# One gelu function at the gMLP projections' eviction, and v's chain ahead of u's half, in a hybrid encoder layer

## The chip, the cores and the metric

The kernel runs on one core of a Trainium2 chip. The metric is the device time of one execution in microseconds (us), the median of three runs. The engines of the core are called as in the profile: PE multiplies matrices (PEld loads its stationary operand), DVE does elementwise work with two operands and reductions, ACT applies functions elementwise with a scale, POOL does small powers here, and SP's queue (SPq) issues nearly all DMAs. Each engine and each queue takes its instructions in the order in which they stand in the program.

## The reference, cut to what matters

Two sequences of 1024 rows go through the same layer. Of the combined projection, two slices of 512 columns, `gu` and `gv`, feed the spatial gating:

```python
def chunked_spatial_gating(u, v, v_gain, w_s, b_s):
    u = jax.nn.gelu(u)                          # the tanh form
    v = rms_norm(jax.nn.gelu(v), v_gain)        # mean over 512 columns
    vh = v.reshape(B, nc, CHUNK, GM_HEADS, GM_HD)
    s = jnp.einsum("hpq,bcqhd->bcphd", w_s, vh) + jnp.transpose(b_s)[None, None, :, :, None]
    return (u.reshape(B, nc, CHUNK, GM_HEADS, GM_HD) * s).reshape(B, S, GM_WIDTH)

    h = rms_norm(x, norm1)
    proj = h @ w_in                             # q, k, v, gu, gv
    a = rms_norm(windowed_gqa(...), attn_out_gain)
    g = rms_norm(chunked_spatial_gating(gu, gv, v_gain, w_s, b_s), gmlp_out_gain)
    x = x + jnp.concatenate([a, g], axis=-1) @ w_o
    h2 = rms_norm(x, norm2)
    x = x + (jax.nn.silu(h2 @ w_gate) * (h2 @ w_up)) @ w_down
```

## The kernel before, in words

The 2048 rows are 16 tiles of 128 rows. The kernel has four stages on the time axis of the profile: the attention with its projections, up to about 300 us; the gMLP loop (`for t in range(NT)`, L805 to L827), to about 472 us; the output projection in eight pairs of tiles, to about 661 us; and the FFN, to the end.

**The gMLP loop.** For each tile t, `gm_pieces(t, 0)` projects v: 24 matmuls (8 blocks of the model dimension by three, since each f32 operand is split into a high and a low part, L221 to L223) into one PSUM bank, which ACT empties with a multiplication by the row's norm (L533) into `xg[t][:, 0]`. `gm_pieces(t, 1)` does the same for u into `xg[t][:, 1]`. Then `gm_chain(t)` works on both halves at once, 1024 columns wide: Square on ACT (L643), two operations on DVE (L644, L645), Tanh on ACT (L646), and on DVE one product each for v (L648) and u (L649, written into the group's tile `us`). That is twice the tanh form of gelu; the factor two is taken out by both norms that follow, whose constant is four times as large. Then v's norm: Square with a sum on ACT (L651), a small operation on DVE (`v_e`, L152), a power on POOL (`v_r`, L156), the scaling on DVE (L653), and the split of v into a high part (casts on ACT, `vh`, L103) and a low part (subtractions on DVE, `vl`, L104).

**The groups.** Four tiles make a group. `gm_group` multiplies by the 128x128 gating matrices: eight PSUM banks `sg0` to `sg7`, one per head, three matmuls each (L664 to L666), each freed by two products on DVE with u (L669). Then come the norm of g (L677, L154, L156, L679) and its store to DRAM (L680, `mix_g`). `sg` shares a pool of four PSUM banks, `xx`, with the transposes `pm` of the output projection and the two small sums `ps_n` (L845) and `ps_es` (L756), so that `sg4` waits until the DVE has freed a bank. The program calls group g at t = 4g + 5; group 3 follows after the loop, beside the first pairs of the output projection.

**Other work in the loop.** `wo_step(k)` and `wo_step2(k)` prepare the output projection's weights for Strassen's seven products: raw tiles `wr` are loaded (L716), scaled (L717), combined (L721 to L724) and split into f16 parts `wo0h`, `wo0l` and so on (L107 on ACT, L108 on DVE). The last tile pair, `wq_0` and `wq_1` (`wo_last`, loaded by L737, split by L115 and L116 into `wo6h` and `wo6l`), needs the slot that `vgs`, v's gain, holds until the last chain has run. `o_turn(0)` (L779 to L803) transposes the first pair's rows and splits their combinations into the operands `mo`; in the loop's last round it stands between v's half and u's half.

**The output projection.** A pair is seven products of 12 matmuls each (L855 to L857, `wa`, `wb`, `wc`, `wd`), with copies to `sc` (ACT L898, L913; DVE L902, L909, L914) and, for a pair's last products, `xr` (L875) between them.

**What sets the order.** In this part no order is written out by hand. The framework's scheduler fixes, when the program is built, in which order each engine takes its instructions; on the chip the engines then only wait for one another. The attention ahead of it is ordered by a table of times (`AT`); projections of v for tiles 0 and 1 (`NFILL`) run there already.

Of the kernel before, what the change touches and what calls it, by code (L numbers as in the profile page):

```python
# [12 lines left out]
AF = mybir.ActivationFunctionType  # L13
ALU = mybir.AluOpType
AX = mybir.AxisListType

P = 128
# [8 lines left out]
GW = 512  # L26
NF = 22
EPS = 1e-6
# [24 lines left out]
def kernel(  # L53
# [33 lines left out]
    def k4(tag, name, shape=(P, D), dt=F32):  # L87
        return k4p.tile(list(shape), dt, tag=tag, name=name, bufs=slots[tag])
# [7 lines left out]
    def mm(name, shape):  # L96
        return psm.tile(list(shape), F32, tag="mm", name=name)
# [427 lines left out]
    def gm_pieces(t, z):  # L525
        nm_ = ("gv", "gu")[z]
        if z == 0:
            pxg[t] = k4("S", f"xg{t}", (P, 2, GW))
        ps = mm(f"p{nm_}{t}", [P, GW])
        for k in range(KD):  # L530
            mm3(ps, hT[t](k), wgl[nm_][0][:, k, :], wgl[nm_][1][:, k, :], k == 0, k == KD - 1)
            yield
        nc.scalar.mul(pxg[t][:, z], ps, rstd1[t])  # L533
        yield

    def run(it, n=None):
        while n is None or n > 0:
            if next(it, "end") == "end":
                return False
            if n is not None:  # L540
                n -= 1
        return True
# [89 lines left out]
    def gm_chain(t):  # L632
        gi, c = divmod(t, GROUP)
        if c == 0:
            grp[gi] = (
                [k4("L", f"u{gi}_{c}", (P, 2, GW)) for c in range(2)],
                [k4("L", f"vh{gi}_{c}", (P, 4, GROUP, HD), F32R) for c in range(2)],
                [k4("L", f"vl{gi}_{c}", (P, 4, GROUP, HD), F32R) for c in range(2)],
            )
        us, vh, vl = grp[gi]  # L640
        xg = pxg.pop(t)
        tt = k4("S", f"tt{t}", (P, 2, GW))
        nc.scalar.activation(tt, xg, AF.Square)  # L643
        nc.vector.tensor_scalar(tt, tt, 0.044715 * SQRT_2_PI, SQRT_2_PI, ALU.mult, ALU.add)  # L644
        nc.vector.tensor_mul(tt, tt, xg)  # L645
        nc.scalar.activation(tt, tt, AF.Tanh)  # L646
        u2 = us[c // 2][:, c % 2, :]
        nc.vector.scalar_tensor_tensor(xg[:, 0], tt[:, 0], 1.0, xg[:, 0], ALU.add, ALU.mult)  # L648
        nc.vector.scalar_tensor_tensor(u2, tt[:, 1], 1.0, xg[:, 1], ALU.add, ALU.mult)  # L649
        ms = small("v_ms", 1)  # L650
        nc.scalar.activation(tt[:, 0], xg[:, 0], AF.Square, scale=1.0 / math.sqrt(GW), accum_out=ms)  # L651
        rv = rsqrt_mean("v", ms, 1, 4.0 * EPS)
        nc.vector.scalar_tensor_tensor(xg[:, 0], xg[:, 0], rv, vgs, ALU.mult, ALU.mult)  # L653
        for z in range(2):
            src = xg[:, 0, z * 256 : (z + 1) * 256].rearrange("p (h d) -> p h d", h=4)
            split(vh[z][:, :, c, :], vl[z][:, :, c, :], src)

    def gm_group(gi):
        us, vh, vl = grp[gi]
        for h in range(NH):  # L660
            ps = xx(f"sg{gi}_{h}", [P, GROUP, HD])
            z, j = divmod(h, 4)
            vhh, vll = vh[z][:, j], vl[z][:, j]
            nc.tensor.matmul(ps, ws_hi[:, h, :], vhh, start=True, stop=False)  # L664
            nc.tensor.matmul(ps, ws_hi[:, h, :], vll, start=False, stop=False)
            nc.tensor.matmul(ps, ws_lo[:, h, :], vhh, start=False, stop=True)  # L666
            for c2 in range(2):
                u2 = us[c2][:, :, h * HD : (h + 1) * HD]
                nc.vector.scalar_tensor_tensor(  # L669
                    u2, ps[:, c2 * 2 : c2 * 2 + 2, :], bss[:, h : h + 1], u2, ALU.add, ALU.mult  # L670
                )
        for c in range(GROUP):
            t = gi * GROUP + c
            g = us[c // 2][:, c % 2, :]
            jk = k4("S", f"gj{t}", (P, GW))
            ms = small("x_ms", 1)
            nc.scalar.activation(jk, g, AF.Square, scale=1.0 / math.sqrt(GW), accum_out=ms)  # L677
            rg = rsqrt_mean("v", ms, 1, 4.0 * EPS, MIX_UP)
            nc.vector.tensor_scalar_mul(jk, g, rg)  # L679
            store(mix_g[t], jk)  # L680

# [122 lines left out]
    for t in range(NT):  # L804
        if t + 1 < NT and t + 1 >= NFILL:  # L805
            split_x(t + 1)
        if t >= NFILL:
            run(gm_pieces(t, 0))
        if t > GROUP and t % GROUP == 1:
            gm_group(t // GROUP - 1)  # L810
            gm_chain(t - 1)
        if t == NT - 1:
            o_turn(0)
        run(gm_pieces(t, 1))
        if 1 <= t < 5:
            wo_sum(2 * t - 2)
            wo_sum(2 * t - 1)
        if t == 5:
            wo_gain()
        if 3 <= t < 11:  # L820
            early_sum(t - 3)
        if t in WO_AT:
            wo_step(WO_AT.index(t))
        if t in WO2_AT:
            wo_step2(WO2_AT.index(t))
        if t == 0 or t % GROUP:
            gm_chain(t)  # L827

    onec = cp.tile([P, P], F32, name="onec")
    nc.gpsimd.memset(onec, 1.0)  # L830
# [670 lines left out]
```

## Time and profile before

| | |
|---|---|
| median of three runs | 1881.17 us (1880.75 to 1884.06) |
| the profiled execution | 1884.11 us, span of the trace 1882.3 us |
| PE busy | 1835.8 us, 98% of the span |
| DVE busy | 1208.1 us, 64% |
| ACT busy | 1036.7 us, 55% |
| POOL busy | 116.2 us, 6% |
| SP's queue (q1) | 280.02 MB, 47.5% of 16 DMA engines |

The span reaches from the first to the last instruction of the profiled execution; 1.8 us of its own time lie around it. The shares are means over four stages with different limits. A row of the timeline has the start, the length, engine, line, operation, output and inputs, shapes and count, and in brackets how long the engine had been idle and what it waited for. Lengths overlap: matmuls follow each other at less than the length of one.

### The profile page before, as it was taken

To read this page: it belongs to the slowest core of one execution; us is meant where nothing else is said; L and a number is where in the kernel's file an instruction comes from. 1 tells how busy PE (TensorE), PEld (TensorE's weight loads), DVE (VectorE), ACT (ScalarE), POOL (GpSimd) and SP (SyncE) were. 2 spreads that over 40 slices of the span, in tenths; PEclk is the share of its full clock that TensorE was granted. 3 is DMA by queue.
4 is the path that set the end of the run, shared out by engine and by line. 5 is a ranking of instruction groups with operands and counts; after the bars stand their busy time and mean duration, and the time that the engine had idled before them with its cause. 6 is when DMAs were issued, how large, how long until landed. Compare 5 with 4: busy or idle time off the path is not lost.

```text
span 1882.3 us, 26161 instructions
## 1 busy us (share of the span) xinstructions
PE 1835.8 (98%) x9696; PEld 997.5 (53%) x9696; DVE 1208.1 (64%) x2243; ACT 1036.7 (55%) x1946; POOL 116.2 (6%) x149
## 2 busy tenths in 40 slices
PE   8999989999899989999999999999999999999999
PEld 7677767878455444444444444444444444444444
DVE  4887876788877878645645645545556856555661
ACT  6798978776576775534534534444344453333340
POOL 3122100111100000000000000000000000000000
PEclk9999989999999999999999999999999999999999
DMA  7798878433377876313313313223263563333641
GB/s 239 150 195 176 180 163 259 142 139 105 124 233 248 278 241 229 118 47 128 122 58 123 113 67 112 84 96 107 75 227 123 212 218 127 120 101 101 227 142 45
DMA packets 216208, 282.06 MB, mean 150 GB/s; under 512 B 103282, under 2 KB 138098, under 8 KB 216080
## 3 DMA queue, kind: packets, MB, share of 16 engines
q1 hardware_dynamic: 215632, 280.02, 47.5%
q8 instruction: 76, 1.25, 0.3%
q14 instruction: 52, 0.43, 0.1%
q0 software_dynamic: 304, 0.10, 0.1%
q10 hardware_dynamic: 144, 0.26, 0.0%
HBM read 177.04 MB, written 80.23 MB: 137 GB/s over the span
## 4 chain that ended last, share of the span: by engine, by line
PE 57%; DVE 2%; DMA 2%; issue 2%; ACT 1%; POOL 0%; SPq 0%; POOLq 0%; DVEq 0%; ACTq 0%
PE pd L1340 7%; PE pd L1338 7%; PE pd L1339 7%; PE pa L1064 4%; PE pa L1066 4%; PE pa L1065 4%; PE pd L1064 4%; PE pd L1066 3%; PE pd L1065 3%; PE pc L1064 3%; PE pc L1066 3%; PE pc L1065 3%; PE pb L1064 2%; PE pb L1065 2%; PE pb L1066 2%
## 5 line engine op out<-in xcount | busy, mean ns | idle before, releaser
L1338 PE MATMUL pd<-wop,a 128*128 128x512 f16 x616 | 234.2, 380 | 2.1 <-ACT a L115 2.1
L1339 PE MATMUL pd<-wop,a 128*128 128x512 f16 x616 | 234.2, 380 | 0.0
L1340 PE MATMUL pd<-wop,a 128*128 128x512 f16 x616 | 233.9, 380 | 0.1
L1065 PEld LDWEIGHTS <-op 128*128 128x128 f16 x1232 | 120.6, 98 | 148.9 <-issue 7.2
L1066 PEld LDWEIGHTS <-op 128*128 128x128 f16 x1232 | 120.6, 98 | 146.5 <-issue 1.4
L1064 PEld LDWEIGHTS <-op 128*128 128x128 f16 x1232 | 122.3, 99 | 143.2 <-issue 0.5
L1064 PE MATMUL pa<-top,op 128*128 128x512 f16 x352 | 133.4, 379 | 1.7 <-ACT ua L1182 1.7
L1066 PE MATMUL pa<-top,op 128*128 128x512 f16 x352 | 133.4, 379 | 0.0
L1065 PE MATMUL pa<-top,op 128*128 128x512 f16 x352 | 133.4, 379 | 0.0
L115 ACT ACTIVATE wop<-wd,wdr_r 128x512 f16<-128x512 f32 x66 | 47.3, 720 | 154.7 <-PE pd L1340 151.6
L115 ACT ACTIVATE a<-as,asr_r 128x512 f16<-128x512 f32 x154 | 102.0, 710 | 33.3 <-DMA as<-act_d 16.3
L116 DVE SCALAR_TENSOR_TENSOR a<-as,asr_r,a 128x512 f16<-128x512 f32 x154 | 108.9, 747 | 8.2 <-ACT a L115 8.1
L116 DVE SCALAR_TENSOR_TENSOR wop<-wd,wdr_r,wop 128x512 f16<-128x512 f32 x66 | 49.2, 750 | 101.1 <-ACT wop L115 101.1
L1193 ACT COPY ub<-pc 128x512 f32<-128x512 f32 x44 | 25.8, 585 | 159.9 <-PE pc L1066 159.9
L1338 PEld LDWEIGHTS <-a 128*128 128x128 f16 x616 | 60.5, 98 | 75.5 <-ACT a L115 2.6
L1340 PEld LDWEIGHTS <-a 128*128 128x128 f16 x616 | 60.3, 98 | 73.4 <-DVE a L116 0.8
L1339 PEld LDWEIGHTS <-a 128*128 128x128 f16 x616 | 60.4, 98 | 72.8 <-issue 0.6
L1007 ACT ACTIVATE junk_e<-g 128x1024 f32<-128x1024 f32 x44 | 46.4, 1054 | 75.0 <-DVE g L1177 75.0
L1199 DVE TENSOR_TENSOR ub<-ub,ua 128x512 f32<-128x512 f32 x44 | 30.4, 692 | 81.6 <-ACT ub L1193 79.2
L439 ACT ACTIVATE sc<-sc,mx 128x384 f32<-128x384 f32 (+1 forms) x128 | 74.5, 584 | 13.2 <-DVE mx L423 12.9
L1174 ACT ACTIVATE g<-g,rs 128x512 f32<-128x512 f32 x57 | 41.1, 722 | 62.5 <-DVE g L1209 35.5
L423 DVE CUSTOM_DVE_ANT_0 sc<-ps,bias 128x384 f32<-128x384 f32 (+1 forms) x128 | 62.4, 520 | 17.2 <-PE ps L418 13.9
(378 smaller groups left out, 4706.5 us busy)
## 6 DMA issues: line engine op xcount, KB each, us to landing
as<-act_d SPq DMA_DIRECT2D x77, 512.0 KB, 3.4
act_d<-g SPq DMA_DIRECT2D x66, 256.0 KB, 2.0
xs<-in_xT_dram SPq DMA_DIRECT2D x28, 512.0 KB, 4.3
tr<-t_d SPq DMA_DIRECT2D x28, 512.0 KB, 4.9
raw<-in_wg_dram SPq DMA_DIRECT2D x24, 512.0 KB, 3.6
raw<-in_wu_dram SPq DMA_DIRECT2D x24, 512.0 KB, 4.5
act_d<-sa SPq DMA_DIRECT2D x44, 256.0 KB, 2.3
act_d<-sb SPq DMA_DIRECT2D x44, 256.0 KB, 2.6
```

The costliest lines, as they stand in the source:

```text
L115: nc.scalar.mul(hi, src, gain)
L116: nc.vector.scalar_tensor_tensor(lo, src, gain, hi, ALU.mult, ALU.subtract)
L423: nc.vector.tensor_tensor_reduce(out=sc[:, v, :W], in0=ps[v][:, :W], in1=bias[:, h, self.off : self.off + W], scale=1.0, scalar=-NEG, op0= ...
L439: nc.scalar.activation(sc[:, v, :W], sc[:, v, :W], AF.Exp, bias=self.mn[:, h : h + 1], scale=-1.0, accum_out=self.sums[:, h : h + 1],)
L1007: nc.scalar.activation(junk_e[0], src, AF.Square, accum_out=acc)
L1064: nc.tensor.matmul(ps, op[:, 0, k, :], th[:, k, :], start=first and k == 0, stop=False, **more)
L1065: nc.tensor.matmul(ps, op[:, 0, k, :], tl[:, k, :], start=False, stop=False, **more)
L1066: nc.tensor.matmul(ps, op[:, 1, k, :], th[:, k, :], start=False, stop=last and k == 3, **more)
L1174: nc.scalar.activation(dst, src, AF.Silu, scale=iv)
L1338: nc.tensor.matmul(ps, a[:, 0, s, cs], wop[:, 0], start=first and n == 0, stop=False, **kw)
L1339: nc.tensor.matmul(ps, a[:, 0, s, cs], wop[:, 1], start=False, stop=False, **kw)
L1340: nc.tensor.matmul(ps, a[:, 1, s, cs], wop[:, 0], start=False, stop=end, **kw)
```

## The change

- The eviction of v and u applies `Gelu_apprx_tanh` with the row's norm as scale, in place of the multiplication alone. The 1024-wide Square, the two DVE operations, Tanh and the two products (L643 to L649) go, and both norms have the plain constant.
- u goes straight into the group's tile `us`. For the first tile of each group, whose group tile does not exist yet, it goes through `xg[:, 1]`, and one copy on DVE brings it over (one for each of four groups).
- v of tiles 0 and 1, evicted within the attention stage, is still multiplied alone there; its gelu comes in the chain, on ACT in place.
- `gm_chain(t)`, which now deals with v alone, stands ahead of the u half of round t, no longer behind it. In the rounds with a group, the group comes first, then the chains of t - 1 and t.

```diff
@@ gm_pieces
         if z == 0:
             pxg[t] = k4("S", f"xg{t}", (P, 2, GW))
+        elif t % GROUP:
+            pxg[t] = grp[t // GROUP][0][t % GROUP // 2][:, t % 2, :]
         ps = mm(f"p{nm_}{t}", [P, GW])
         for k in range(KD):
             mm3(ps, hT[t](k), wgl[nm_][0][:, k, :], wgl[nm_][1][:, k, :], k == 0, k == KD - 1)
             yield
-        nc.scalar.mul(pxg[t][:, z], ps, rstd1[t])
+        if z:
+            dst = pxg[t] if t % GROUP else pxg[t][:, 1]
+            nc.scalar.activation(dst, ps, AF.Gelu_apprx_tanh, scale=rstd1[t])
+        elif t < NFILL:
+            nc.scalar.mul(pxg[t][:, 0], ps, rstd1[t])
+        else:
+            nc.scalar.activation(pxg[t][:, 0], ps, AF.Gelu_apprx_tanh, scale=rstd1[t])
         yield
@@ gm_chain
         xg = pxg.pop(t)
-        tt = k4("S", f"tt{t}", (P, 2, GW))
-        nc.scalar.activation(tt, xg, AF.Square)
-        nc.vector.tensor_scalar(tt, tt, 0.044715 * SQRT_2_PI, SQRT_2_PI, ALU.mult, ALU.add)
-        nc.vector.tensor_mul(tt, tt, xg)
-        nc.scalar.activation(tt, tt, AF.Tanh)
-        u2 = us[c // 2][:, c % 2, :]
-        nc.vector.scalar_tensor_tensor(xg[:, 0], tt[:, 0], 1.0, xg[:, 0], ALU.add, ALU.mult)
-        nc.vector.scalar_tensor_tensor(u2, tt[:, 1], 1.0, xg[:, 1], ALU.add, ALU.mult)
+        if t < NFILL:
+            nc.scalar.activation(xg[:, 0], xg[:, 0], AF.Gelu_apprx_tanh)
         ms = small("v_ms", 1)
-        nc.scalar.activation(tt[:, 0], xg[:, 0], AF.Square, scale=1.0 / math.sqrt(GW), accum_out=ms)
-        rv = rsqrt_mean("v", ms, 1, 4.0 * EPS)
+        tt = k4("S", f"tt{t}", (P, GW))
+        nc.scalar.activation(tt, xg[:, 0], AF.Square, scale=1.0 / math.sqrt(GW), accum_out=ms)
+        rv = rsqrt_mean("v", ms, 1, EPS)
+        if c == 0:
+            nc.vector.tensor_copy(us[0][:, 0, :], xg[:, 1])
@@ the loop
         if t >= NFILL:
             run(gm_pieces(t, 0))
+        if t % GROUP:
+            if t == 1:
+                gm_chain(0)
+            if t % GROUP != 1 or t == 1:
+                gm_chain(t)
         if t > GROUP and t % GROUP == 1:
             gm_group(t // GROUP - 1)
             gm_chain(t - 1)
+            gm_chain(t)
         if t == NT - 1:
             o_turn(0)
         run(gm_pieces(t, 1))
...
-        if t == 0 or t % GROUP:
-            gm_chain(t)
```

Behind the change the line numbers are five to nine higher: L664 to L666 become L669 to L671, L669 becomes L674, L653 becomes L658, L837 and L847 become L846 and L856, L759 to L763 become L764 to L768, L855 to L857 become L864 to L866. The order of the two programs differs at three places that matter below.

On PE behind the last tile's u half, before: group 3's first matmuls stand inside the first pair's fourth product (`wc`), behind 40 of that pair's matmuls.

```order
L855 MATMUL wc_6303<-wo3h,mo_1_6020 128x512
L664 MATMUL sg_0_6107<-vh_0_5810,ws_hi 128x256
L664 MATMUL sg_1_6113<-vh_0_5810,ws_hi 128x256
L664 MATMUL sg_2_6119<-vh_0_5810,ws_hi 128x256
L664 MATMUL sg_3_6125<-vh_0_5810,ws_hi 128x256
L856 LDWEIGHTS mo_1_6020
L856 MATMUL wc_6303<-wo3l,mo_1_6020 128x512
```

The same place now, where `ps_n` follows directly on the last u matmul (L223):

```order
L854 MATMUL ps_n_6001<-m,onec 128x1
L761 MATMUL ps_es<-kss,onec 128x8
L669 MATMUL sg_0_6017<-vh_0_5743,ws_hi 128x256
L670 MATMUL sg_0_6017<-vl_0_5745,ws_hi 128x256
L671 MATMUL sg_0_6017<-vh_0_5743,ws_lo 128x256
L864 LDWEIGHTS mo_0_5947
L864 MATMUL wa_6118<-wo0h,mo_0_5947 128x512
L669 MATMUL sg_1_6023<-vh_0_5743,ws_hi 128x256
```

Group 3 has moved ahead of the first pair's products, and the small sums' banks and `sg`'s are asked for within a few matmuls.

On DVE at the same place, behind the last split of the first pair's operands (`mo_3`), before: the chain of tile 15 (`tt_6068`, `xg_5961`) runs among the small sums.

```order
L108 TENSOR_TENSOR mo_3_6022<-sc_6018,mo_3_6022 128x512
L644 TENSOR_SCALAR tt_6068<-tt_6068 128x1024
L837 TENSOR_SCALAR n_e<-ps_n_6091 128x1 x2
L645 TENSOR_TENSOR tt_6068<-tt_6068,xg_5961 128x1024
L847 TENSOR_SCALAR n2s<-n2s,n_r 128x8
L759 TENSOR_REDUCE es_er<-ps_es 128x4
L760 TENSOR_SCALAR es_er<-es_er 128x4
L762 TENSOR_TENSOR es_er<-es_er 128x4
```

And now:

```order
L108 TENSOR_TENSOR mo_3_5950<-sc_5946,mo_3_5950 128x512
L846 TENSOR_SCALAR n_e<-ps_n_6001 128x1 x2
L764 TENSOR_REDUCE es_er<-ps_es 128x4
L674 SCALAR_TENSOR_TENSOR u_0_5741<-sg_0_6017,bss,u_0_5741 128x2x64
L856 TENSOR_SCALAR n2s<-n2s,n_r 128x8
L765 TENSOR_SCALAR es_er<-es_er 128x4
L674 SCALAR_TENSOR_TENSOR u_1_5742<-sg_0_6017,bss,u_1_5742 128x2x64
L767 TENSOR_TENSOR es_er<-es_er 128x4
L674 SCALAR_TENSOR_TENSOR u_0_5741<-sg_1_6023,bss,u_0_5741 128x2x64
```

The products that free `sg0` and `sg1` now alternate with the steps of the two small sums, which wait for powers on POOL (between L846 and L856, and between L765 and L767).

On DVE ahead of group 1's products (round t = 9), before: the last step of the preparation of k = 1 (`wr_5222` is its tile wr5) stands there.

```order
L723 TENSOR_TENSOR wr_5222<-wr_5222,wr_5221 128x512
L108 TENSOR_TENSOR wo3l<-wr_5221,wo3h 128x512
L724 TENSOR_TENSOR wr_5222<-wr_5222 128x512
L108 TENSOR_TENSOR wo1l<-wr_5222,wo1h 128x512
L108 TENSOR_TENSOR wo4l<-wr_5221,wo4h 128x512
L108 TENSOR_TENSOR wo5l<-wr_5222,wo5h 128x512
L669 SCALAR_TENSOR_TENSOR u_0_4889<-sg_0_5276,bss,u_0_4889 128x2x64
```

And now, where `wr_5450` and `wr_5451` are the tiles wr2 and wr6 of k = 2:

```order
L108 TENSOR_TENSOR wo5l<-wr_5178,wo5h 128x512
L108 TENSOR_TENSOR wo0l<-wr_5450,wo0h 128x512
L726 TENSOR_TENSOR wr_5450<-wr_5450 128x512
L727 TENSOR_TENSOR wr_5450<-wr_5451,wr_5450 128x512
L108 TENSOR_TENSOR wo4l<-wr_5450,wo4h 128x512
L108 TENSOR_TENSOR wo2l<-wr_5451,wo2h 128x512
L728 TENSOR_TENSOR wr_5451<-wr_5451,wr_5450 128x512
L674 SCALAR_TENSOR_TENSOR u_0_4868<-sg_0_5232,bss,u_0_4868 128x2x64
```

The preparation of k = 1 has moved ahead, and group 1's products now stand behind the first part of k = 2, which needs wr2 and wr6 to be loaded.

## Rows read from the trace of the kernel before

**Rows 1.** What PE waited for, 300 to 600 us (in total, times, longest)

```profile
PE sg L664 <- ACT vh L103: 3.1, 1, 3.1
PE sg L664 <- DVE u L669: 2.8, 1, 2.8
PE wd L855 <- ACT wo6h L115: 2.2, 1, 2.2
```

**Rows 2.** Windows: length, busy us of each engine, PEclk (granted clock), DMA share, GB/s

```profile
390.00:400.00 10.00, 7.56 (x32) 6.68 (x33) 8.23 (x24) 6.06 (x12) 0.86 (x1) 0.83 0.32 121
484.00:490.00 6.00, 6.00 (x31) 5.17 (x32) 4.73 (x17) 1.59 (x3) 0.00 (x0) 0.72 0.27 89
500.00:507.00 7.00, 6.13 (x20) 2.37 (x20) 6.15 (x11) 3.72 (x7) 0.00 (x0) 0.76 0.40 145
```

**Rows 3.** Groups by line: busy us, mean ns of one, idle before

```profile
L645 DVE TENSOR_TENSOR tt<-tt,xg 128x1024 f32<-128x1024 f32 x16 | 19.6, 1223 | 0.3
L1174 ACT ACT_TABLE_LOAD x1 | 1.3, 1283 | 0.0
```

**Rows 4.** Timeline of ACT at tile 0's u half and at tile 15's chain

```profile
295.95 0.69 ACT L533 ACTIVATE xg<-pgu,rstd_all 128x512 f32<-128x512 f32 x1 [2.12 <-PE pgu L223]
...
481.11 0.63 ACT L651 ACTIVATE tt<-xg 128x512 f32<-128x512 f32 x1 [2.79 <-DVE xg L648]
```

**Rows 5.** Timeline of PE from tile 15's v to the first pair's end

```profile
463.75 1.91 PE L779 MATMUL pm<-ident,mix 128*128 128x128 f32 x16
...
470.99 0.28 PE L845 MATMUL ps_n<-m,onec 128*128 128x1 f32 x2
...
484.00 0.74 PE L664 MATMUL sg<-vh,ws_hi 128*128 128x256 f32 x4 [3.15 <-ACT vh L103]
...
489.64 0.28 PE L665 MATMUL sg<-vl,ws_hi 128*128 128x256 f32 x1
489.76 0.28 PE L666 MATMUL sg<-vh,ws_lo 128*128 128x256 f32 x1
...
506.58 0.38 PE L855 MATMUL wb<-wo1h,mo 128*128 128x512 f16 x1
...
509.17 1.91 PE L779 MATMUL pm<-ident,mix 128*128 128x128 f32 x16
```

**Rows 6.** Timeline of DVE around the loop's end

```profile
467.35 0.75 DVE L653 SCALAR_TENSOR_TENSOR xg<-xg,v_r,vgs 128x512 f32<-128x512 f32 x1 [0.73 <-POOL v_r L156]
...
472.88 2.49 DVE L108 TENSOR_TENSOR mo<-sc,mo 128x512 f16<-128x512 f32 x4
...
475.88 0.22 DVE L837 TENSOR_SCALAR n_e<-ps_n 128x1 f32<-128x1 f32 x2
...
477.83 0.23 DVE L847 TENSOR_SCALAR n2s<-n2s,n_r 128x8 f32<-128x8 f32 x1 [0.59 <-POOL n_r L838]
...
479.46 0.16 DVE L762 TENSOR_TENSOR es_er<-es_er 128x4 f32<-128x4 f32 x1 [1.13 <-POOL es_er L761]
```

**Rows 7.** Timeline of POOL at the same place

```profile
476.18 1.61 POOL L838 TENSOR_TENSOR n_r<-n_e,pm 128x2 f32<-128x2 f32 x1 [8.87 <-DVE n_e L837]
```

**Rows 8.** DMA issues, 455 to 512 us: KB each, median us from issue to landing

```profile
wq<-in_w_o_dram SPq DMA_DIRECT2D x2, 512.0 KB, 4.6
```

**Rows 9.** Timeline around group 1, and two loads of raw weights

```profile
391.25 0.88 SPq L716 DMA_DIRECT2D wr<-in_w_o_dram  x2
391.68 3.20 DVE L669 SCALAR_TENSOR_TENSOR u<-sg,bss,u 128x128 f32<-128x128 f32 x12
...
394.70 1.15 ACT L717 ACTIVATE wr<-wr,wgain 128x1024 f32<-128x1024 f32 x1 [3.49 <-DMA wr<-in_w_o_dram]
...
420.98 0.33 SPq L716 DMA_DIRECT2D wr<-in_w_o_dram  x1
...
425.48 1.16 ACT L717 ACTIVATE wr<-wr,wgain 128x1024 f32<-128x1024 f32 x1 [1.45 <-DMA wr<-in_w_o_dram]
```

**Rows 10.** Timeline of PE in the FFN, one wait

```profile
704.25 0.38 PE L1064 MATMUL pd<-top_6h,op 128*128 128x512 f16 x1 [1.14 <-ACT ub L1197]
```

More of the change, by code (lines that the diff above doesn't have):

```diff
@@ L677, in gm_group @@
             nc.scalar.activation(jk, g, AF.Square, scale=1.0 / math.sqrt(GW), accum_out=ms)
-            rg = rsqrt_mean("v", ms, 1, 4.0 * EPS, MIX_UP)
+            rg = rsqrt_mean("v", ms, 1, EPS, MIX_UP)
             nc.vector.tensor_scalar_mul(jk, g, rg)
```

## The prediction

> **What bounds the kernel now.** I read the table of busy time first: PE works for 98% of the span, DVE for 64%, ACT for 55%. So an operation taken from ACT or DVE is worth nothing by itself. L645 alone is 19.6 us of DVE [rows 3], and ACT and DVE lose several such groups, but all of it lies beside PE's matmuls. What counts is where PE stands still, or runs at a lower clock, because of what the change touches. So I read next what PE waited for between 300 and 600 us [rows 1]. Three waits stand out there: 3.1 us in group 3, for the high part of v; 2.8 us in group 1, for DVE's product that frees a bank of `sg`; 2.2 us in the first pair's last product, for `wo6h`. Then the windows [rows 2]: each wait comes with a stretch in which the granted clock falls to 0.83, 0.72 and 0.76, that is, a part of it is at the lower of two levels, 1.2 GHz for 2.4. A part x at half speed makes a mean of 1 - x/2, so 0.72 over 6 us is 3.4 us at half clock and 0.76 over 7 us is 3.4 us too; work at half clock takes twice its time, so each costs about 1.7 us; 0.83 over 10 us is 3.4 us, 1.7 us also. The rest of the 1.8 ms the change leaves as it is.
>
> **The change part by part.**
>
> *Group 3 and the first pair.* This is the term that decides. In before, u of tile 15 ends and `ps_n` starts at 470.99; the second pair's second product begins at 506.58 [rows 5]: 35.6 us. The work in it is 96 f16 matmuls, 24 of `sg`, 16 transposes and the small sums. Twelve f16 matmuls take from 506.58 to 509.17, 0.216 each, so 96 make 20.7; an `sg` matmul takes 0.12 (489.64 to 489.76), 24 make 2.9; the transposes 1.9; the sums 0.5. That is 26.0, so 9.6 us are lost. Rows 1 and 2 give 3.15 + 2.2 + 1.7 + 1.7 = 8.8 of it; the rest is a 0.6 us wait at `ps_es` and rounding.
>
> The 3.15 us comes from the chain of tile 15: it starts behind u's half, passes DVE twice, and its Square L651 starts only at 481.11 [rows 4]; 2.9 us later `vh` is ready and PE goes on at 484.00 [rows 5]. Now the chain starts when v's half ends, 463.75 (the transposes start there). Gelu takes 0.68 (as L533) [rows 4], and from Square to ready 2.9 plus two L108 that stand ahead of the low parts; so v is ready at about 469, two us before u ends at 471. **This wait goes**, and its half-clocked stretch with it.
>
> What takes its place: the order now puts group 3 directly behind u. `sg0` to `sg3` need banks of the pool that `pm`, `ps_n` and `ps_es` use, and `sg4` and `sg5` need those that L674 frees. On DVE, L674 for `sg0` and `sg1` stands among the two small sums, and DVE waits twice there for POOL: the power of `n_r` takes 1.61 us [rows 7], and `es_er`'s makes DVE wait 1.13 [rows 6]. I lay it out from before's lengths. `mo_3`'s split ends at 475.37 (472.88 + 2.49) in before; now v's eviction, Square, sum and power run from 463.75 end to end and the scaling starts about 1.25 earlier than L653's 467.35 [rows 6], and the operations behind it follow on: 474.1. Then L846 and the reduction, then the first L674, then 1.6 of waiting for POOL until L856 (476.1), then `sg0`'s second product: its bank is free at about 476.75. PE has finished what stands ahead of `sg4` at 475.35: **1.4 us new wait**. `sg5` needs the second power (1.0 to 1.13): free at 478.55, PE there at 477.55: **1.0 us**. `ps_es` keeps 0.1 of its wait.
>
> The 2.2 us for `wo6h` goes too. `wq_1` waits for the slot that `wq_0` leaves. In before the chain of tile 15 holds `vgs` until late; its scaling is now done at about 467, so `wq_0` is issued there, and `wq_1` behind `wq_0`'s last split, about 483.3; 4.6 us later [rows 8] it lands, 487.9. PE asks for `wo6h` after 491. But the splits now stand ahead of other work: ACT's L115 ahead of the copy L909, DVE's L116 ahead of L875. Worked out the same way, PE meets these with 1.2 us in hand, and L898 behind them 0.1 late: **0.1 us**.
>
> Sum: 9.6 - (0.1 + 1.4 + 1.0 + 0.1) = 7.0 us. Its weakest part is the clock behind the two new waits. A wait of 1.14 us in the FFN (at 704.25) [rows 10] is followed by matmuls at full clock, one of 2.2 by a slow stretch [rows 1, 2]. Each of the new ones is nearer to the first, so I take no dip; one dip costs 1.7. If `wq_1` lands 1.1 us later than the median, another 1.3 to 1.6 is lost.
>
> *Group 1.* In before L669 starts at 391.68, right behind the split of k = 1 [rows 9], and PE loses 2.8 to the wait and 1.7 to the clock. In after, the preparation of k = 1 stands earlier, which would free L674, but that of k = 2 has come ahead of it, as far as L728, and so the load of wr6. I estimate its time from before's steps: the lighter DVE is done with k = 1 some 5 to 6 us earlier, at about 383; the load is issued there and takes 3.45 to 4.5 (391.25 to 394.70, 420.98 to 425.48) [rows 9]; then a scaling and five DVE steps. That puts L674 at about 391.7 again, by chance the old place, and the wait at 3.6, as PE comes 0.8 earlier: PE's end of the stretch is unchanged. **Zero**, between -4.5 (the wait of 2.8 and the clock's 1.7 both go: the load early) and +2 (a load as slow as the slowest, twice in turn).
>
> *Groups 0 and 2* cost PE no wait in before, and their chains only get shorter: zero. The copy of u for a group's first tile, four times on DVE, lies in its idle time.
>
> *The table.* Gelu needs another function table than Exp: one ACT_TABLE_LOAD more. The one for Silu took 1283 ns [rows 3]. The new one comes at the first gelu, shortly ahead of 295.95, where ACT had been idle for 2.12 us [rows 4]: covered, zero. The cover gone, 1.3 us on ACT, of which PE sees a part at most. The Trainium skill (page "ScalarE: Activation LUTs", section "What ACT_TABLE_LOAD costs") adds a drain of about as much again, so that a switch is some 2.66 us; that would overrun the idle time by 0.5 us, and the forecast would be 1874.7 at most. No row here shows a drain on its own.
>
> *Gelu's rate.* No gelu runs in before. The nearest row is the multiplication it replaces, 0.69 us for 512 columns [rows 4]. Below that it can't go by more than a few hundredths, which the bound of 0.63 of the Square beside it shows; if it took twice that, 32 evictions would give back some 22 us of ACT, off PE's path but for 0.7 in group 3's chain, which has 2 us in hand. Zero.
>
> **Sum.** The profiled execution is 1884.11, 2.94 above the median; 7.0 less is 1877.1 by its own time, and on the median's basis 1881.17 - 7.0 = **1874.2 us**.
>
> **The rivals.** *Larger gain: group 1's wait goes too.* For it speaks that ACT and DVE are lighter everywhere, so that all preparation may run further ahead than my 5 to 6 us; against it, that wr6's load waits for a slot. It gives 1874.2 - 4.5 = 1869.7. *Smaller gain: a new wait takes the old one's place in group 3.* The two waits for POOL, 2.4 us close together, may act on the clock like one of 2.2 [rows 1, 2]: 1.7, and `wq_1` a little late, 1.5. It gives 1874.2 + 3.2 = 1877.4, and with a slow load in group 1 1879.4, within 0.2% of before. 0.2%, 3.8 us, is about what a measurement of this kernel can tell from no change. *Slower: DVE's queue behind wr6.* L674 of group 1 stands behind steps that need wr6; in before nothing there waited for a load issued so late. Every microsecond that wr6 lands later than 387.3 PE waits longer. With group 3's gain as forecast, it breaks even at 7 us late (394.4) and is over 0.2% slower from 11 us on; at 12 us it gives 1886. Against it: the two loads in rows 9 differ by 1 us, and the queue carries little there, 0.32 of its capacity [rows 2]. *It doesn't do what it says*: v's chain is ready only behind `o_turn`'s work on ACT, so that PE waits at `sg0`; each us costs a us, and 2 us are in hand. I count it with the smaller gain.
>
> **How the numbers follow.** The forecast 0.52 (1872 to 1877), the larger gain 0.15, the smaller 0.20, the slower rival 0.07, others 0.06 spread over both sides. The range holds the forecast, the smaller gain with its slow load and the larger gain: 1869 to 1880.5. Faster by over 0.2% (below 1877.4): the forecast, the larger gain and a part of the smaller and of the others, 0.70; within 0.2%: 0.21; slower: 0.09.
>
> **What would show it.** In the changed kernel's trace: the row of PE waiting for `vh` in group 3 gone; `sg4` and `sg5` waiting 1.4 and 1.0 for L674; no wait for `wo6h`; 470.99 to 506.58 shortened from 35.6 to about 28.6; a granted clock near 1 in the first pair's windows; L674 of group 1 at about 391.7 with 3.6 us of wait. The forecast is wrong if a clock dip follows the two waits, if group 1's wait differs by more than 2 us, or if the scaled time of one part outside the loop (attention, FFN) has moved, for which the change gives no reason.

## The result and the profile after

The changed kernel takes 1871.19 us (median of 4 runs, 1869.51 to 1873.22) against 1882.24 us (4 runs): a ratio of 0.9942, 95% interval 0.9927 to 0.9958, 11 us less. A second, larger set of runs gave medians of 1873.49 and 1883.3 and a ratio of 0.9953 (0.9937 to 0.9970), 9 to 10 us less. So the forecast, 7 us less, was right in its direction and somewhat small: 1871.19 lies just below the 1872 to 1877 that stood for the forecast itself, on the side of the larger gain.

The table of busy time of the changed kernel (share of the span 1868.1, instructions):

```profile
PE 1827.9 (98%) x9696; PEld 994.0 (53%) x9696; DVE 1160.2 (62%) x2183; ACT 1007.8 (54%) x1917; POOL 109.2 (6%) x149
```

DVE lost 47.9 us of work and ACT 28.9, and the kernel got 11 us faster: the shares say nothing of the gain. What PE waited for between 300 and 600 us (in total, times, longest) does, beside [rows 1]:

```profile
PE pm L784 <- DMA mix<-mix_a: 2.7, 1, 2.7
PE sg L669 <- ACT wo1h L107: 2.3, 1, 2.3
PE sg L669 <- DVE u L674: 0.9, 2, 0.6
```

Of the three waits of [rows 1] those for `vh` (3.1) and for `wo6h` (2.2) are gone. The wait of 2.8 in group 1 is now 2.3; the profile names the ACT cast that ended last before it, but the row behind it shows that it was DVE's L674 (below). The wait for `mix` belongs to a later pair and stands before as well, there behind 600 us: from 500 to 720 us PE waits for it 3.9 and 4.7 us in the two traces of the kernel before, 4.4 and 4.8 in the two of the changed one. Group 3, on PE, in the timeline:

```profile
467.76 0.40 PE L223 MATMUL pgu<-wgu_hi,xl 128*128 128x512 f32 x1
467.99 0.28 PE L854 MATMUL ps_n<-m,onec 128*128 128x1 f32 x2
468.13 0.37 PE L761 MATMUL ps_es<-kss,onec 128*128 128x8 f32 x2
468.46 0.36 PE L669 MATMUL sg<-vh,ws_hi 128*128 128x256 f32 x1
...
472.97 0.36 PE L669 MATMUL sg<-vh,ws_hi 128*128 128x256 f32 x1 [0.26 <-DVE u L674]
...
474.66 0.36 PE L669 MATMUL sg<-vh,ws_hi 128*128 128x256 f32 x1 [0.65 <-DVE u L674]
...
495.50 0.38 PE L864 MATMUL wb<-wo1h,mo 128*128 128x512 f16 x1
```

From `ps_n` to the second pair's second product is now 27.5 us (467.99 to 495.50) for 35.6 [rows 5]. That is 8.1 us, where the prediction had 7.0. `sg0` starts without a wait, and `sg4` and `sg5` wait 0.26 and 0.65 where 1.4 and 1.0 were forecast.

The windows around group 1 and around the first pairs (length, busy us of each engine, granted clock, DMA share, GB/s), first of the kernel before:

```profile
386.00:402.00 16.00, 12.76 (x60) 10.74 (x59) 13.79 (x35) 10.12 (x20) 2.26 (x3) 0.89 0.41 147
468.00:508.00 40.00, 34.14 (x161) 19.55 (x161) 33.04 (x75) 19.06 (x38) 6.14 (x7) 0.91 0.30 101
```

and of the changed one:

```profile
386.00:402.00 16.00, 13.72 (x72) 11.76 (x71) 13.31 (x37) 9.84 (x21) 3.69 (x5) 1.00 0.23 74
468.00:508.00 40.00, 39.09 (x211) 21.88 (x210) 33.81 (x77) 24.57 (x51) 5.41 (x8) 1.00 0.47 164
```

The clock stays at its upper level in both. To set traces side by side, two stretches are read from each, as differences of the starts of two PE instructions: group 1, from its first `sg` matmul to that of group 2, and group 3, from the last matmul of u to the first `wb` matmul of the second pair (0.2 us more than the 35.6 above, as it starts one matmul earlier). The last column is the ratio to the kernel before with its interval.

| kernel | group 1 | group 3 | ratio |
|---|---|---|---|
| before | 51.7 | 35.8 | |
| before, second trace | 51.7 | 36.5 | |
| changed | 48.9 | 27.7 | 0.9942 (0.9927 to 0.9958) |
| changed, second set and trace | 51.6 | 27.7 | 0.9953 (0.9937 to 0.9970) |
| gelu alone, chain behind u | 51.6 | 27.3 | 0.9947 (0.9929 to 0.9965) |
| move, old formula in two halves | 52.7 | 30.3 | 0.9998 (0.9986 to 1.0010) |
| tile 15's chain behind u | 50.8 | 27.3 | 0.9941 (0.9920 to 0.9961) |
| gelu for v alone | 48.2 | 28.5 | 0.9937 (0.9922 to 0.9953) |
| gelu for tile 15 alone, chain behind u | 51.9 | 30.5 | 0.9982 (0.9972 to 0.9992) |
| gelu for tile 15 alone, chain ahead | 51.4 | 29.7 | 0.9974 (0.9960 to 0.9988) |
| small sums early | 48.7 | 26.1 | 0.9949 (0.9934 to 0.9964) |
| weights behind group 1 | 46.4 | 27.8 | 0.9918 (0.9902 to 0.9933) |
| both of these | 46.9 | 26.1 | 0.9914 (0.9897 to 0.9930) |

Outside these stretches the traces of one and the same kernel differ by a few us (from the second pair to the FFN 154.9 and 155.7 in the two of before, 153.3 and 154.7 in the two of the changed kernel; the loop's first group of `sg` starts between 335.7 and 340.1 in all of them). So of the 14 us between the two profiled executions, only the 8 us of group 3 repeat. Group 1 adds between 0 and 3 us: five traces have the changed kernel's order there (changed, its second trace, gelu alone, tile 15's chain behind u, small sums early), and their stretch is 48.7 to 51.6, in the mean 50.3 for 51.7. What makes up the rest of the 9 to 11 us is not shown.

### The profile page after: what moved, and what is told of

It is laid out like the page before. It is cut to its first block, busy times and chain, and to the rows that moved or that the text cites. A ratio compares the mean times of both kernels' runs of the same rounds, so it can differ in the third digit from the quotient of the medians.

```text
span 1868.1 us, 26075 instructions
## 1 busy us (share of the span) xinstructions
PE 1827.9 (98%) x9696; PEld 994.0 (53%) x9696; DVE 1160.2 (62%) x2183; ACT 1007.8 (54%) x1917; POOL 109.2 (6%) x149
## 3 DMA queue, kind: packets, MB, share of 16 engines
q1 hardware_dynamic: 215632, 280.02, 47.9%
## 4 chain that ended last, share of the span: by engine, by line
PE 58%; DVE 2%; DMA 2%; issue 2%; ACT 1%; POOL 0%; POOLq 0%; SPq 0%; DVEq 0%; ACTq 0%
PE pd L1349 7%; PE pd L1347 7%; PE pd L1348 7%; PE pa L1073 4%; PE pa L1075 4%; PE pa L1074 4%; PE pd L1073 4%; PE pd L1074 4%; PE pd L1075 4%; PE pc L1073 4%; PE pc L1074 4%; PE pc L1075 4%; PE pb L1073 2%; PE pb L1074 2%; PE pb L1075 2%
## 5 line engine op out<-in xcount | busy, mean ns | idle before, releaser
L115 ACT ACTIVATE wop<-wd,wdr_r 128x512 f16<-128x512 f32 x66 | 47.3, 720 | 154.2 <-PE pd L1349 151.2
L1016 ACT ACTIVATE junk_e<-g 128x1024 f32<-128x1024 f32 x44 | 46.4, 1053 | 74.2 <-DVE g L1186 74.2
```

The lines of the kernel that those rows point to most:

```text
L115: nc.scalar.mul(hi, src, gain)
L1016: nc.scalar.activation(junk_e[0], src, AF.Square, accum_out=acc)
```

## The experiments

**The changed kernel once more.**

> The changed kernel once more, as the yardstick for the others and for a second trace. Both theories: about 11 us below the kernel before (ratio 0.994). The rows that the explanation rests on must repeat: group 1's sg waiting about 2.3 us for the product that frees a bank, with no half-clocked matmuls behind it; group 3's two waits of 0.3 and 0.7 us; 27.5 us from the loop's last sum to the first pair's end. What the first trace gained behind 506 us (3 us) should not repeat if it was only clock dips of that one profile of before.

Measured: 1873.49 us, 0.9953. The two waits in group 3 came back as 0.25 and 0.65. Group 1 did not repeat. Its windows in this trace:

```profile
386.00:402.00 16.00, 12.61 (x56) 10.64 (x55) 12.52 (x36) 9.14 (x21) 3.70 (x5) 0.89 0.23 79
468.00:508.00 40.00, 39.10 (x211) 21.93 (x210) 33.77 (x76) 24.55 (x51) 5.42 (x8) 1.00 0.48 167
```

and PE's wait in it:

```profile
389.65 0.36 PE L669 MATMUL sg<-vh,ws_hi 128*128 128x256 f32 x1 [3.39 <-ACT wo1h L107]
```

The wait is 3.4 us, the clock falls to 0.89 behind it as in the kernel before, and group 1's stretch is 51.6, the length that it had in the kernel before. The 2.8 us that the first trace gained there are no part of the change that can be counted on.

**Gelu alone.** All chains stand behind u's half again:

```diff
-        if t % GROUP:
-            if t == 1:
-                gm_chain(0)
-            if t % GROUP != 1 or t == 1:
-                gm_chain(t)
         if t > GROUP and t % GROUP == 1:
             gm_group(t // GROUP - 1)
             gm_chain(t - 1)
-            gm_chain(t)
...
+        if t == 0 or t % GROUP:
+            gm_chain(t)
```

> The gelu function alone: v's chain (short now, v only) stands behind u's half again, in all rounds. Theory, the short chain is most of the gain: tile 15's v comes about 4 us later than in the changed kernel, but no DVE step and no Tanh stand in its way, so group 3 loses 4 to 5 us to waits where the changed kernel loses 1, and group 1 loses 0.6 more; wo6h is still on time. 6 us below before, ratio 0.997 (0.996 to 0.998). Rival, the move ahead of u's half is the whole of it: PE waits 3 us for vh, 2 for wo6h and dips follow; within 3 us of before, ratio 0.9985 to 1.0.

Measured: 1872.24 us, 0.9947, as the changed kernel; the theory's 4 to 5 us of loss in group 3 did not come. What PE waited for, 300 to 600 us:

```profile
PE sg L669 <- DVE u L674: 3.4, 1, 3.4
...
PE sg L670 <- DVE vl L104: 0.8, 1, 0.8
```

The second row is all that group 3 loses. The scheduler has put eleven matmuls of the first pair's first product between the small sums and `sg0`, and ACT's cast of v's high part ends just as they do:

```profile
470.07 0.71 ACT L103 CAST vh<-xg 128x256 fp32r<-128x256 f32 x2 [1.53 <-DVE xg L658]
```

and PE takes it up at once, to wait for the low part:

```profile
470.52 0.62 PE L669 MATMUL sg<-vh,ws_hi 128*128 128x256 f32 x3
471.93 0.39 PE L670 MATMUL sg<-vl,ws_hi 128*128 128x256 f32 x1 [0.79 <-DVE vl L104]
```

In the kernel before, 40 matmuls stood there and still 3.15 us were missing. So the theory, in which the chain's new place saves some 4 us, falls, and the rival, in which the move is everything, falls further.

**The move with the old formula.** v's chain stands ahead of u's half; v and u each have Square, two DVE operations, Tanh and a product (512 wide). So it is not the move by itself: the one 1024-wide chain has become two, with more instructions on DVE. The edit, shown against the changed kernel:

```diff
-        if t < NFILL:
-            nc.scalar.activation(xg[:, 0], xg[:, 0], AF.Gelu_apprx_tanh)
+        tt = k4("S", f"tt{t}", (P, 2, GW))
+        twice_gelu(tt[:, 0], xg[:, 0], xg[:, 0])
...
+        if t % GROUP:
+            gm_uchain(t)
```

> The move alone: v's chain stands ahead of u's half, but gelu is still made of Square, two DVE operations, Tanh and a product, for v and u apart (512 columns each). Theory, the move is the smaller part: group 3's wait for vh goes, but DVE has the longer chains of v and u in between, so that group 3's products and the first pair's operands come 1 to 3 us later than in the changed kernel; group 1 is as before or worse (DVE has more instructions than before). 3 to 6 us below before, ratio 0.997 to 0.9985. Rival, the move alone gives all: 10 us below, ratio 0.994 to 0.995.

Measured: 0.9998, no difference at all, less than either theory gave it. Group 3's stretch is 5.5 us shorter (30.3), but PE now waits elsewhere:

```profile
PE pgv L223 <- DVE xl L191: 5.6, 4, 3.0
PE ps_w L703 <- POOL ones L701: 2.1, 1, 2.1
PE ps_es L763 <- DVE mo L108: 1.6, 1, 1.6
PE wd L870 <- ACT sc L928: 1.3, 1, 1.3
```

No row for `vh` is left: the move, too, takes that wait away. `xl` is the low part of x, which each tile's projection needs. DVE computes it in L191, in the same queue as the chains; that their two sets of 512-wide operations hold it back is argued from this order, not tested. The stretches from group 0 to group 1 (51.0 for 47.3), group 1 (52.7 for 51.7) and from group 2 to u's end (32.6 for 31.9) lose 5.4 us together and give back what group 3 gained. Of the first stretch's 3.7 us, 1.8 lie at `ps_w` (2.1 for 0.3), which waits for POOL.

**Tile 15's chain alone behind u.** Like the kernel with all chains late, but for the last tile only.

```diff
-            if t % GROUP != 1 or t == 1:
+            if t % GROUP != 1 and t < NT - 1 or t == 1:
                 gm_chain(t)
...
+        if t == NT - 1:
+            gm_chain(t)
```

> The changed kernel with the chain of tile 15 alone behind u's half. Both agree that groups 0 to 2 stay (group 1's wait 2.3 us). Theory, the move pays in group 3 only: 3.5 to 4.5 us above the changed kernel, all of it between the loop's last sum and the first pair's end (31 to 32 us for 27.5), the waits at vh and vl of sg0 to sg2. Rival, the move pays in the other rounds too: this kernel is nearer to the changed one than to the kernel with all chains late.

Measured: 0.9941, group 3 in 27.3 (group 1's wait 2.8 us, its stretch 50.8). The theory's loss isn't there, and since the kernel with all chains late is as fast as the changed one, the rival has nothing left to tell apart. Where the chain is one function long, its place in the last round is worth nothing.

**Gelu for v alone.** u keeps the long form (`gm_uchain` as above), v's chain is that of the changed kernel.

> The changed kernel with gelu as one function for v alone; u keeps Square, two DVE operations, Tanh and a product, 512 wide, behind its half. Theory A, v's short chain is what pays: group 3 gains as in the changed kernel but for u of tile 15, whose chain of about 5 us holds the banks of sg0 to sg2; stretch 29 to 31 us for 27.75; group 1 as in the kernel before; ratio 0.995 to 0.9975. Theory B, what pays is DVE's and ACT's relief as such, and half of it is given back: PE waits for the low part of x in several rounds, as it did where the old formula was split in halves; ratio 0.998 to 1.0.

Measured: 0.9937, as the changed kernel. Group 3 takes 28.5, 0.8 more: nearer to theory A, though milder than its 29 to 31, and with 1.1 us of waiting in the sixth product and 0.4 at one `sg` in place of the banks of `sg0` to `sg2`. Of theory B one wait for `xl` is there, 1.4 us. The ratio is better than A gave it, since in this kernel's order group 1's products stand ahead of k = 2's weights, as in the kernel before, and no `sg` matmul waits there (stretch 48.2 us, with the 1.4 us for `xl` in it). So what u's gelu gains in group 3 goes again by the other order in group 1: the gelu of u, half of the work that was removed, brings nothing that the times can tell.

**Gelu for tile 15 alone**, first with its chain where the kernel before has it:

```diff
+        if t == NT - 1:
+            nc.scalar.activation(pxg[t][:, z], ps, AF.Gelu_apprx_tanh, scale=rstd1[t])
+        else:
+            nc.scalar.mul(pxg[t][:, z], ps, rstd1[t])
```

> The kernel before, with gelu as one function for tile 15 alone (v and u, at their evictions; its chain stays behind u's half, fifteen tiles keep Square, two DVE operations, Tanh and two products). Theory, the short chain of the one tile on which group 3 waits is nearly all of the gain: u's end to the first pair's end 27 to 29.5 us for 35.8, no wait for vh and none for wo6h; group 1 as before (first sg of group 1 to first sg of group 2 51 to 52 us); 6 to 8 us below before, ratio 0.9957 to 0.997. Rival, the relief of DVE and ACT by all sixteen tiles is needed, since DVE reaches the loop's end late: the stretch stays above 32 us, ratio above 0.998.

Measured: 0.9982 (3.2 us by the medians), group 3 in 30.5, 5.3 less, between the theory and the rival. The wait for `vh` is 0.3; what is left is in other rows:

```profile
PE wd L861 <- ACT sc L919: 2.3, 1, 2.3
PE ps_es L762 <- DVE sc L802: 1.2, 1, 1.2
```

The first of them is the sixth product's: the scaling of v ran at 476.14, so `wq_0` was issued at 476.92 and `wq_1` only at 485.86, and `wo6h` was made from 492.29 on; ACT's copy L919, which the row names, stands behind it in ACT's queue. SP's queue:

```profile
476.92 0.38 SPq L743 DMA_DIRECT2D wq<-in_w_o_dram  x1
...
485.86 1.09 SPq L743 DMA_DIRECT2D wq<-in_w_o_dram  x1
```

and ACT's row:

```profile
492.29 1.33 ACT L115 ACTIVATE wo6h<-wq,wgain 128x512 f16<-128x512 f32 x2 [1.94 <-DMA wq<-in_w_o_dram]
```

Then with that chain ahead of u's half (`gm_chain(t)` in front of `o_turn(0)` for t = 15, u straight into the group's tile):

> The kernel before, with gelu as one function for tile 15 alone, and that tile's chain ahead of its u half (the other fifteen tiles as in the kernel before). In the same kernel with the chain behind u, u's end to the first pair's end was 30.5 us, with 2.3 us of waiting in the sixth product, since wq_1 was issued only when tile 15's scaling had let go of v's gain. Theory: the scaling is now some 7 us earlier, wq_1 lands in time, that wait goes, and the stretch is that of the changed kernel, 27.5 to 29 us; ratio 0.9955 to 0.997, so one tile gives all that can be told of the change. Rival, fifteen long chains keep DVE late at the loop's end and the products of group 3 wait for it: stretch 30 us or more, ratio 0.998 as with the chain behind u.

Measured: 0.9974 (5.5 us by the medians), group 3 in 29.7, outside the theory's bands and just below the rival's 30. `wq_0` is issued at 469.32 and `wq_1` at 484.81, and the sixth product's wait falls from 2.3 to 0.8; `ps_es` still waits 1.35, since tile 14's long chain makes DVE late with the first pair's operands (its scaling runs at 467.00, tile 15's behind it at 468.54). So the one tile gives 6.1 us of group 3's 8.1, and the other 2 come from the fifteen tiles ahead of it, in which alone the two kernels differ.

**The small sums early.** In the changed kernel, `n_r` and `es_er` with their matmuls and powers go into round 12:

```diff
+        if t == 12:
+            n2ss = small("m", 1)
...
+            n2r = norm_pair("n2", ps_n2, H_NORM**-2)
+            nc.vector.tensor_scalar_mul(n2s, n2s, n2r[:, 0:1])
+            early_scale()
```

> The changed kernel with the two small sums (n_r and es_er, with their matmuls and powers) moved into round 12, where DVE is idle. Theory, what is left of waiting at sg4 and sg5 in group 3 (0.26 and 0.65 us) is DVE waiting for POOL between its products: both waits go or fall below 0.3, the stretch from u's end to the first pair's end is 26.5 to 27.0 us for 27.75; too little for the times, ratio 0.994 to 0.995. Rival, the banks are late because DVE ends the first pair's splits late: the waits stay.

Measured: of the two waits one is gone and 0.2 us of the other are left. The stretch is 26.1, 1.6 less than in the changed kernel, as part of the sums' own work left it too. DVE's products now follow each other behind the splits:

```profile
467.29 1.28 DVE L108 TENSOR_TENSOR mo<-sc,mo 128x512 f16<-128x512 f32 x2
468.49 1.64 DVE L674 SCALAR_TENSOR_TENSOR u<-sg,bss,u 128x128 f32<-128x128 f32 x6
```

The times can't tell this from the changed kernel, as expected.

**The weights behind group 1.** A small step on DVE makes the scale of k = 2 and 3 depend on group 1's last product:

```diff
+        if t == 10:
+            u_end = grp[1][0][1][:, 1, GW - KD :]
+            nc.vector.scalar_tensor_tensor(wgain_b, u_end, 0.0, wgain, ALU.mult, ALU.add)
...
-            nc.scalar.mul(r, r, wgain[:, j : j + 1])
+            nc.scalar.mul(r, r, (wgain if k < 2 else wgain_b)[:, j : j + 1])
```

> The changed kernel, but the weight preparation of k = 2 and 3 can't pass group 1: its scale is a copy of wgain that one small DVE step makes behind the last product of group 1. Theory, group 1's products stand behind steps that need wr6, and that alone holds PE: DVE has been idle since about 382, the bank comes free when sg0 is done, the wait of 2.3 to 3.4 us and its half-clocked matmuls go: from group 1's first sg to group 2's first 46 to 48 us for 48.9 to 51.7; 2 to 5 us below the changed kernel, ratio to before 0.992 to 0.9935. Rival, the queue only moves: the preparation of k = 2 and 3 starts 5 us later and meets group 2's products or the first pair, which lose as much; ratio as the changed kernel, 0.9945 to 0.995.

Measured: 1867.47 us, 0.9918: 4 to 6 us below the two medians of the changed kernel. Group 1's wait is gone, DVE takes the products as soon as `sg0` is there (its first `sg` matmul starts at 382.72), and the clock stays up. DVE's row:

```profile
383.27 4.22 DVE L674 SCALAR_TENSOR_TENSOR u<-sg,bss,u 128x128 f32<-128x128 f32 x16 [6.20 <-PE sg L671]
```

The window of group 1:

```profile
386.00:402.00 16.00, 16.00 (x74) 13.28 (x73) 10.61 (x30) 12.63 (x28) 4.20 (x7) 1.00 0.27 100
```

DVE had been idle for 6.2 us ahead of it. No wait came up in group 2; in group 3 the same 0.9 us stayed. The rival falls.

**Both.**

> Both of the two edits before: the preparation of k = 2 and 3 behind group 1, and the small sums in round 12. If both theories hold, the gains add: 3 to 6 us below the changed kernel, ratio 0.9915 to 0.993. If the queue only moves, as the changed kernel or 1 us below it.

Measured: 1865.85 us, 0.9914. In the trace both gains stand (46.9 and 26.1); in the times the second is too small to be told. This is the best version: 17.5 us below the kernel before by the medians.

**The kernel before, a second trace.**

> The kernel before, for a second trace. If the explanation holds: u's end to the first pair's end 35.8 us within 1 us, with the waits for vh (3.1) and wo6h (2.2); group 1's first sg to group 2's first 51 to 52 us; behind 506 us up to 2 us less or more, as the granted clock falls or not behind the loads of mix.

Measured: 1883.99 us in one run; group 3 in 36.5 with waits of 3.15 and 2.92, group 1 in 51.7. The stretches that the explanation rests on repeat; the wait of 2.92 is that for `wo6h`, 2.2 in the first trace.

## Why the prediction was right, point by point

**What bounds.** The reading that an operation off PE's path is worth nothing by itself, and that three waits and the clock behind them are what can be won, held: half of the removed work (u's) brings nothing that the times can tell, and the chain of one tile pays 6.1 of group 3's 8.1 us.

**The wait for vh.** That it goes, and its half-clocked stretch with it, was right. What it could not tell is which of the two edits does it: it let the chain start "when v's half ends" and priced both together. With the chain behind u, v's high part is ready at 470.8 (the cast above), 3.1 us behind `ps_n` at 467.65, and the scheduler fills that with eleven matmuls; what took 13.0 us in before (470.99 to 484.00) [rows 5] was the length of the chain, its passes through DVE behind other work and through Tanh. Either edit takes the wait away. With the short chain, moving it was not needed; moved with the old formula, it shortened group 3 by 5.5 us and lost as much elsewhere.

**The two new waits.** The mechanism was right, the size was not, and this is the term of the sum that missed most: 0.26 and 0.65 for 1.4 and 1.0. The rows, DVE:

```profile
471.24 0.21 DVE L846 TENSOR_SCALAR n_e<-ps_n 128x1 f32<-128x1 f32 x2
471.37 0.15 DVE L764 TENSOR_REDUCE es_er<-ps_es 128x4 f32<-128x8 f32 x1
471.45 0.34 DVE L674 SCALAR_TENSOR_TENSOR u<-sg,bss,u 128x128 f32<-128x128 f32 x1
472.27 0.23 DVE L856 TENSOR_SCALAR n2s<-n2s,n_r 128x8 f32<-128x8 f32 x1 [0.48 <-POOL n_r L847]
...
473.70 0.16 DVE L767 TENSOR_TENSOR es_er<-es_er 128x4 f32<-128x4 f32 x1 [0.87 <-POOL es_er L766]
```

and POOL:

```profile
471.53 0.70 POOL L847 TENSOR_TENSOR n_r<-n_e,pm 128x2 f32<-128x2 f32 x1 [8.26 <-DVE es_er L764]
472.65 1.01 POOL L766 TENSOR_TENSOR es_er<-es_er,nhalf 128x4 f32<-128x4 f32 x1 [0.42 <-DVE es_er L765]
```

DVE waits twice for POOL with products behind it, as forecast, but the first power took 0.70 us, where [rows 7] has 1.61 for the same instruction, and the second wait is 0.87 for 1.13. The splits ended at 471.24, 3.2 us behind `ps_n`; forecast was 3.1 (474.1 less 470.99). The sum's 2.6 us of new losses became 0.9; of these 1.7 us, 1.1 are the excess of the gain (8.1 over 7.0), and 0.6 lie in gaps too small for a row. No dip followed these waits (the granted clock is 1.00 from 468 to 508), as chosen. Why the same power is shorter here stays open, and nothing in the prediction foresaw it. That the sums stand in the way at all is shown by the kernel that has them early.

**wo6h.** Right: no row for it is left. `wq_0` is issued at 464.09, where the prediction, moved by the 3 us that the loop ends earlier, has 463.9; `wq_1` at 479.70 for 480.3. The kernels with gelu in one tile show the same chain from v's gain to `wo6h` with a wait of 2.3 and 0.8 at its end.

**Group 1.** "Zero" is what the second trace shows (-0.1); the first has -2.8, and the five traces with this order have -1.4 in the mean. The order it was read from was right: DVE's products stand behind k = 2. The wait was 2.3 and 3.4 for the forecast 3.6, and L674 began 3.1 and 4.2 us behind the group's first `sg` (4.6 was forecast). The rows of ACT and DVE, first trace:

```profile
386.66 1.15 ACT L722 ACTIVATE wr<-wr,wgain 128x1024 f32<-128x1024 f32 x1 [0.86 <-DMA wr<-in_w_o_dram]
...
390.26 4.21 DVE L674 SCALAR_TENSOR_TENSOR u<-sg,bss,u 128x128 f32<-128x128 f32 x16
```

and second trace:

```profile
385.30 1.15 ACT L722 ACTIVATE wr<-wr,wgain 128x1024 f32<-128x1024 f32 x1 [2.21 <-DMA wr<-in_w_o_dram]
...
388.90 3.83 DVE L674 SCALAR_TENSOR_TENSOR u<-sg,bss,u 128x128 f32<-128x128 f32 x14
```

What decides is when wr6 has landed compared with when PE arrives: ACT scales wr6 0.5 us ahead of the first `sg` (387.14) in the first trace and 0.6 behind it (384.67) in the second, and PE waits 1.1 us more there. The load was issued 5.4 and 5.6 us ahead of that `sg`, and ACT had the tile 4.9 and 6.3 us after the issue, where the prediction reckoned with 3.45 to 4.5: the same program, a slower load. The kernels with tile 15's chain behind u and with the small sums early fit in: ACT starts 0.1 us behind and 1.3 ahead of the first `sg`, and PE waits 2.8 and 1.5. That this queue is the cause is shown by the kernel which takes the weights behind the products. The 4.5 us of the rival "larger gain" were thus there to be won, but by holding the weights back, not by letting them run further ahead as the rival had it; the change does not reach them.

**The table.** Covered, as forecast. ACT in the changed kernel:

```profile
293.12 1.28 ACT L651 ACT_TABLE_LOAD   x1
294.41 0.63 ACT L651 ACTIVATE xg<-xg 128x512 f32<-128x512 f32 x1
```

The load comes at v's gelu in tile 0's chain, not in the idle time ahead of u's eviction; PE waits for nothing of ACT's between 285 and 330 us. The first gelu starts 0.01 us behind the load's end and the load 0.02 behind the operation ahead of it. The drain that the Trainium skill (page "ScalarE: Activation LUTs", section "What ACT_TABLE_LOAD costs") adds to a switch is not to be seen in these rows, and the measurement decides: 1.28 us here.

**Gelu's rate.** As the multiplication that it replaced, by the groups of ACT's operations (busy us, mean ns, idle before):

```profile
L541 ACT ACTIVATE xg<-pgv,rstd_all 128x512 f32<-128x512 f32 x14 | 9.5, 679 | 14.3 <-PE pgv L223 14.3
L537 ACT ACTIVATE u<-pgu,rstd_all 128x512 f32<-128x512 f32 x12 | 8.1, 678 | 2.6 <-PE pgu L223 2.6
```

0.68 us for 512 columns; the multiplication took 0.69 [rows 4].

**The slower rival** did not come: wr6 was never late enough. What stays open is the difference of 3 us by which the changed kernel's first trace also ran faster behind the second pair's second product (1372.6 us to the end for 1375.7, half of it in the FFN); its second trace does not have it (1376.5), and nothing here ties it to the change.

## What to carry to other kernels

An operation taken from an engine that waits most of the time pays only where it shortens the one chain that PE stands still for: here the last tile before the next stage, 6 of the 8 us for one tile of sixteen. Where a scheduler fixes the order, moving a step in the program text may be worth nothing once the step is short, since other work is put in front of it anyway; and in the order that it makes for lighter queues, other work may slip ahead of what PE waits for, which one false dependence can forbid (4 to 6 us more here). Price a stretch from two traces of the same program before a gain of 3 us is credited to an edit.

## What the runs showed of the hardware

- Whether the granted clock falls behind a wait in group 1 went with the wait's length: behind 2.3 us (the changed kernel's first trace) it stayed at 1.00 in the window 386 to 402, behind 2.8 (before) and 3.4 (the changed kernel's second trace) it was 0.89, a mean over 16 us of which a part is at the lower level. With no wait it was 1.00. The other traces agree: 1.00 behind 1.5 (small sums early), 0.89 behind 2.8 (tile 15's chain behind u) and 3.4 (gelu alone). Between the two traces of the changed kernel 1.1 us of waiting more cost 2.7 us in all.
- The same POOL power on 128 x 2 elements took 1.61 us in the kernel before [rows 7] and 0.70 in the changed one, and so again in the second trace of each (1.62 and 0.70); with gelu for v alone it took 1.08. What sets it is not shown.
- A load of 128x1024 f32 weights, issued at the same place of the same program, was scaled by ACT 4.9 us after its issue in one trace and 6.3 in the other, ACT having waited for it in both.
- The first `sg` matmul starts anywhere between 335.7 and 340.1 in these traces; most of that spread is there already where the first u half starts (283.2 to 286.9), ahead of the chains that the change touches. What makes it is not shown.
